# A hybrid decoder block on one core: the first 512 feed-forward features by plain products, earlier loads of f, and two pad tiles that shift operand addresses

## The chip, the core and the metric

The kernel runs on one core of one Trainium2 chip. The metric is the device time of one execution in microseconds (us); lower is better. Times of the kernel before are given as the median of three executions, and one further execution was taken with the hardware profiler. A difference of under about 0.5% of the time cannot be told from no change.

## The reference, cut to what matters

One decoder layer over 512 positions with 2048 features. A state-space mixer and an attention mixer make `y`; the part that the change touches is the channel mixer behind them:

```
x = x + gt1 * (y @ w_out)
h = rmsnorm(x, g_ffn) * (1 + sc2) + sh2
f = (silu(h @ w_gate) * (h @ w_up)) @ w_down      # w_gate, w_up: 2048 x 5632; w_down: 5632 x 2048
x = x + gt2 * f
return rmsnorm(x, g_final)
```

`sh1, sc1, gt1, sh2, sc2, gt2` come from `silu(c) @ w_mod + b_mod`, a matrix of 2048 x 12288 that is read once. Everything is float32. Products are made of two-part operands: each number is written as `hi + lo`, both in the type fp32r, and a product is hi·hi + hi·lo + lo·hi, three matmuls in one PSUM group.

## The kernel before, in words

All activations lie transposed, with 128 features on the partitions and the 512 positions in the row. A **piece** is 128 x 1024 weights: a DMA from the SP queue fetches it (512 KB), ACT writes its `hi` (a cast, 128x1024), DVE writes its `lo` (a subtraction, 128x1024). Five raw buffers (`wraw`) and three pairs of hi/lo buffers (`whl`) go round. TensorE (PE) then does 24 matmuls with a piece of a plain product: 8 tiles of 128 outputs, three matmuls each, with 512 moving columns (lines 190 to 192).

The instructions of each engine are not issued in the order of the text: the framework's scheduler takes, per engine, what is ready, in order of priority, and `high_priority(30)` lifts the splitting of weights. Each engine then runs its list in that fixed order.

**Stage 1, to `run()` at L1119.** w_in (64 pieces), w_glu (8) and w_out (32) are multiplied by `hA`/`hB`, `vv` and `ys`. Beside them DVE does the state-space work, attention, and the product with `w_mod` (L313, one 512 KB DMA `mraw` for each step). `residual` (L1074) adds the w_out product into `x1`, and the 16 tiles of `x1` are stored to DRAM (`x1d`, L1128) to be read back at the end.

**The seam to stage 2.** From the sum of squares, two small PE steps (L361, L379) and a Newton iteration on DVE make the row `r`; ACT copies it to `rbc` (L1214). For each of 16 tiles, DVE (L1225) and ACT (L1226) make the raw `h` in `rawh`. The channel mixer then works on quadrants, 8 tiles by 256 positions: `b11`, `b21`, `b22` are split at once (L1220, L1221), while `t1` to `t4` are sums of quadrants over 128x2048 (L1237 to L1243), split after that.

**Stage 2, gate and up.** 44 blocks (22 groups of 256 features, gate and up) are done by the seven products of a Strassen-Winograd scheme (p1 to p7, in the order p1 p6 p5 p7 p2 p4 p3). A product is 24 matmuls with 256 moving columns (L1273 to L1275), so there are 44 x 7 x 24 = 7392. p1, p2, p3 move `b11`, `b21`, `b22`; p4 to p7 move `t4`, `t1`, `t2`, `t3`. DVE builds the sums of weight quarters (L1188 to L1194) and recombines; `done` (L1279) multiplies silu(gate) by up, splits it in `fo` and stores it to DRAM (`fd`, L1288).

**Stage 3, w_down.** Two passes of 8 output tiles over 44 tiles of f: 88 pieces, 2112 matmuls of 512 columns. Each `f` tile is read back from `fd` by SP (L1336). The last third of the product with w_mod (GT2, 32 steps) runs beside it, one step for each piece, and `x_back` (L1365) reads `x1` again. The last lines scale and store the output.

**Where operands lie.** Pools of `side="right"` are stacked downward from byte 229,344 of each partition, which is 32 modulo 64; the others upward from the left. Pool sizes are multiples of 64 there, so in the program before, `hA`, `hB`, `vv`, `ys`, `b11`, `b21`, `b22` (right) start at 32 modulo 64, and `t1` to `t4`, `f` and all weight tiles `hi`, `lo` (left) at 0 modulo 64.

## Time and profile before

| | us |
|---|---|
| median of 3 executions (lowest, highest) | 2246.65 (2239.68, 2248.37) |
| the profiled execution: its own time | 2242.28 |
| its span, first to last instruction | 2240.2 |
| mean granted TensorE clock | 0.976 |

The profile's page gives busy times, a strip of 40 slices (56 us each) with the busy tenths of each engine and the granted clock, and the costliest groups of instructions. Other views are the windows (busy time, counts and clock between two instants), the timeline (start, duration, instruction, and in brackets the engine's idle time before it with what ended it), and the DMA list. Matmuls are pipelined: a matmul's own duration overlaps the next one's, so the time that one costs is the distance from start to start, or a window divided by its count.

### The profile page before, as it was taken

The numbers are of one execution on the slowest core, as the hardware profiler recorded it, in microseconds if no ns is written. First come the engines' busy times: TensorE is split into PE (matmuls) and PEld (weight loads), VectorE is DVE, ScalarE is ACT, GpSimd is POOL, SyncE is SP. The second block draws the span as 40 slices with busy tenths as digits, with TensorE's granted clock in tenths as the row PEclk, the third lists the DMA queues.
The fourth block names the chain that finished last, engine by engine and source line by source line (L and its number), as shares of the span: only waits on it lengthen the run. The fifth ranks groups of instructions, "written<-read, shape, count | busy, mean of one in ns | idle before, by whom it ended". The sixth has DMA issues, their size and how long they took to land.

```text
span 2240.2 us, 32899 instructions
## 1 busy us (share of the span) xinstructions
PE 2111.2 (94%) x13032; PEld 1879.8 (84%) x13032; DVE 1556.9 (69%) x2275; ACT 864.5 (39%) x1243; POOL 2.0 (0%) x7
## 2 busy tenths in 40 slices
PE   5999999899999929999999999999997999999996
PEld 3878887677777829999999999999997888888885
DVE  7896868967888688788787887878877344232225
ACT  4432443366743254444444444444443121122111
POOL 0000000000000000000000000000000000000000
PEclk9999989999999959999999999999999999999998
DMA  9989786678887404334343343433435988555552
GB/s 358 331 338 178 230 254 196 215 253 277 305 271 266 161 15 131 120 127 141 125 144 121 130 142 123 147 119 130 141 123 196 353 291 303 194 193 191 195 177 75
DMA packets 196561, 435.94 MB, mean 195 GB/s; under 512 B 50036, under 2 KB 70900, under 8 KB 196408
## 3 DMA queue, kind: packets, MB, share of 16 engines
q1 hardware_dynamic: 196168, 433.13, 58.4%
q8 instruction: 102, 1.67, 0.3%
q0 software_dynamic: 240, 0.72, 0.1%
q14 instruction: 51, 0.42, 0.1%
HBM read 380.38 MB, written 53.41 MB: 194 GB/s over the span
## 4 chain that ended last, share of the span: by engine, by line
PE 70%; DVE 10%; DMA 4%; issue 1%; ACT 1%; SPq 0%; DVEq 0%; ACTq 0%
PE g L190 9%; PE g L192 9%; PE g L191 9%; PE y L1273 6%; PE y L1275 6%; PE y L1274 6%; PE z L1273 4%; PE z L1275 4%; PE z L1274 4%; PE x L1275 4%; PE x L1273 4%; PE x L1274 4%; DMA mraw<-in_w_mod 2%; DVE mraw L313 1%; DVE lo L164 1%
## 5 line engine op out<-in xcount | busy, mean ns | idle before, releaser
L164 DVE TENSOR_TENSOR lo<-raw,hi 128x1024 fp32r<-128x1024 f32 x192 | 236.0, 1231 | 348.9 <-ACT hi L160 343.6
L160 ACT CAST hi<-raw 128x1024 fp32r<-128x1024 f32 x192 | 201.7, 1051 | 580.8 <-PE g L191 399.9
L1273 PE MATMUL y<-btt,hi 128*128 128x256 f32 x1056 | 300.0, 284 | 31.9 <-ACT hi L1176 31.5
L1274 PE MATMUL y<-btt,hi 128*128 128x256 f32 x1056 | 299.6, 284 | 0.0
L1275 PE MATMUL y<-btt,lo 128*128 128x256 f32 x1056 | 299.4, 284 | 0.0
L1176 ACT CAST hi<-raw 128x1024 fp32r<-128x1024 f32 x176 | 184.8, 1050 | 285.3 <-PE x L1274 131.7
L190 PE MATMUL g<-f,hi 128*128 128x512 f32 x704 | 275.2, 391 | 12.7 <-DMA f<-fd 12.7
L313 DVE SCALAR_TENSOR_TENSOR mraw<-mraw,cb 128x1024 f32<-128x1024 f32 x192 | 234.1, 1228 | 70.1 <-DMA mraw<-in_w_mod 69.8
L191 PE MATMUL g<-f,hi 128*128 128x512 f32 x704 | 275.0, 391 | 0.0
L192 PE MATMUL g<-f,lo 128*128 128x512 f32 x704 | 274.8, 390 | 0.0
L1177 DVE TENSOR_TENSOR lo<-raw,hi 128x1024 fp32r<-128x1024 f32 x176 | 215.2, 1223 | 80.2 <-ACT hi L1176 80.0
L1273 PEld LDWEIGHTS y<-btt,hi 128*128 128x128 f32 x1056 | 203.0, 192 | 32.5 <-ACT hi L1176 31.8
L1176 ACT CAST hi<-s 128x1024 fp32r<-128x1024 f32 x132 | 138.9, 1053 | 180.9 <-PE y L1274 92.0
L1275 PEld LDWEIGHTS y<-btt,lo 128*128 128x128 f32 x1056 | 203.4, 193 | 0.0
L1274 PEld LDWEIGHTS y<-btt,hi 128*128 128x128 f32 x1056 | 203.4, 193 | 0.0
L1273 PE MATMUL x<-bab,hi 128*128 128x256 f32 x704 | 198.7, 282 | 3.2 <-ACT bab L1220 3.2
L1275 PE MATMUL x<-bab,lo 128*128 128x256 f32 x704 | 199.0, 283 | 0.0
L1274 PE MATMUL x<-bab,hi 128*128 128x256 f32 x704 | 197.6, 281 | 0.9 <-DVE bab L1221 0.9
L1177 DVE TENSOR_TENSOR lo<-s,hi 128x1024 fp32r<-128x1024 f32 x132 | 161.0, 1220 | 12.9 <-ACT hi L1176 12.4
L190 PEld LDWEIGHTS g<-f,hi 128*128 128x128 f32 x704 | 132.8, 189 | 40.7 <-issue 12.9
L192 PEld LDWEIGHTS g<-f,lo 128*128 128x128 f32 x704 | 132.9, 189 | 27.7
L191 PEld LDWEIGHTS g<-f,hi 128*128 128x128 f32 x704 | 132.9, 189 | 27.5
(291 smaller groups left out, 4408.3 us busy)
## 6 DMA issues: line engine op xcount, KB each, us to landing
mraw<-in_w_mod SPq DMA_DIRECT2D x192, 512.0 KB, 6.2
raw<-in_w_gate SPq DMA_DIRECT2D x88, 512.0 KB, 3.4
raw<-in_w_up SPq DMA_DIRECT2D x88, 512.0 KB, 3.9
raw<-in_w_down SPq DMA_DIRECT2D x88, 512.0 KB, 3.8
f<-fd SPq DMA_DIRECT2D x88, 512.0 KB, 3.3
raw<-in_w_in SPq DMA_DIRECT2D x64, 512.0 KB, 5.7
fd<-fo SPq DMA_DIRECT2D x44, 512.0 KB, 4.6
raw<-in_w_out SPq DMA_DIRECT2D x32, 512.0 KB, 5.1
```

The lines of the kernel that those rows point to most:

```text
L160: ACT.copy(hi, p["raw"])
L164: tt(p["hl"][1], p["raw"], p["hl"][0].bitcast(F32), op=ALU.subtract)
L190: PE.matmul(ps, lhs[0], rhs[0], start=first, stop=False)
L191: PE.matmul(ps, lhs[0], rhs[1], start=False, stop=False)
L192: PE.matmul(ps, lhs[1], rhs[0], start=False, stop=last)
L313: stt(raw, raw, 1.0, cb[:, h * (D // 2):(h + 1) * (D // 2)], op0=ALU.mult, op1=ALU.mult, accum_out=macc[:, m, h:h + 1])
L1176: ACT.copy(hi, raw)
L1177: tt(lo, raw, hi.bitcast(F32), op=ALU.subtract)
L1273: PE.matmul(o, hi[:, sl], bh[:, k], start=f, stop=False, skip_group_check=True)
L1274: PE.matmul(o, hi[:, sl], bo[:, k], start=False, stop=False, skip_group_check=True)
L1275: PE.matmul(o, lo[:, sl], bh[:, k], start=False, stop=l, skip_group_check=True)
```

## The change

It has five parts.

1. **Plain products for the first 512 features.** Groups 0 and 1 of gate and up (four of the 44 blocks) leave the Strassen-Winograd list (`NW = 2`). In their place eight PSUM banks collect four tiles of 128 gate features and four of up, over all 16 tiles of h: 16 x 24 = 384 matmuls with 512 moving columns, tile by tile as `h3(k)` makes h. The moving operand is two runs of 256 columns, one from each quadrant, because h is written straight into quadrants `b11`, `b12`, `b21`, `b22`. Each piece comes by four DMAs of 128 KB with rows of 512 bytes.
2. **h and its sums.** `h3` computes from `r` in PSUM (for the first two tiles), writes `hi`, `lo` and, over `x1`, the raw h. `t1`, `t2`, `t4` have tiles of their own; `t3` takes the place of `b12`. The sums and splits stand in the text behind the plain products, but depend on h alone (and `t3` on the plain products of the first eight tiles).
3. **Stores of x1** move into `residual`, four tiles in one DMA.
4. **Stage 3 starts ahead.** Seven loads of f, three pieces of w_down and two of their splits are placed among the last four Strassen products, in the space of `t1` and `t2`. `x_back` moves from entry 4 to entry 35 of the list, behind the GT2 steps.
5. **Addresses.** A tile of 32 bytes (`edge`) at the right end and further ones (`bpad`, `fpad`) shift what is stacked on the right: `hA`, `hB`, `vv`, `ys` come to 0 modulo 64, `f`, now on the right, stays at 0, and all quadrants and `t1` to `t4` are at 32 modulo 64.

The diff, cut to its core:

```diff
+    ctx.enter_context(tc.tile_pool(name="edge", bufs=1, side="right")).tile([P, 8], F32, name="edge")
...
-    mraw = mrx.enter_context(tc.tile_pool(name="mraw", bufs=MR, reuse_waits="tile"))
+    mraw = mrx.enter_context(tc.tile_pool(name="mraw", bufs=MR, side="right", reuse_waits="tile"))
...
             if half:
+                SP.dma_start(x1v[:, fs_[0]:f + 1], x1[0][:, fs_[0]:f + 1])
                 start(sumsq4(ssq, [x1[0][:, f] for f in fs_], cb_ == 0), 1)
...
-    for k in range(KT):
-        SP.dma_start(x1v[:, k], x1[0][:, k])
...
+    def wk_load(k):
...
+        for j, w in enumerate((w_gate, w_up)):
+            for i in range(NW):
+                SP.dma_start(v[:, j, i], w[i, kh, :, :, kk * P:(kk + 1) * P].rearrange("f p c -> p f c"))
...
+    for k in range(4):
+        wk_load(k)
+    r = rsq_psum(ssq, D)
+    wk_prep(0)
+    wk_prep(1)
...
+    open_banks(g=8)
...
+    bb = [bp.tile([P, 2, 2, H, TH], F32R, name=f"b{i}") for i in range(2)]
+    bp.tile([P, 8], F32, name="bpad")
...
+    def h3(k):
...
+        stt(t, x1[0][:, k], gs2[:, k:k + 1], r if k < 2 else rbc, op0=ALU.mult, op1=ALU.mult)
+        hi, lo = [x[:, kh, :, kk] for x in bb]
+        tv = t.rearrange("p (a t) -> p a t", a=2)
+        ACT.activation(hi, tv, AF.Identity, bias=sh)
+        stt(lo, tv, sh, hi.bitcast(F32), op0=ALU.add, op1=ALU.subtract)
+        ACT.activation(x1[0][:, k], t, AF.Identity, bias=sh)
...
-    for i in range(NB):
+    for i in range(NW, NB):
...
+    for k in range(KT):
+        wk_prep(k + 2)
+        if k + 4 < KT:
+            h3(k + 4)
+        if k == KT - 1:
+            prep(0)
...
+        for m in range(8):
+            sl = slice(m * P, (m + 1) * P)
+            mm3(ps[m], (hi[:, sl], lo[:, sl]), (bh, bo), k == 0, k == KT - 1)
+    sg = []
+    for m in range(4):
+        sg.append(st())
+        ACT.activation(sg[m], ps[m], AF.Silu)
+    for m in range(4):
+        tt(sg[m], ps[4 + m], sg[m], op=ALU.mult)
...
+    for m in range(4):
...
+        SP.dma_start(fd[m, :, :S], hi)
+        SP.dma_start(fd[m, :, S:], sg[m])
...
     for n, (bl, p) in enumerate(items):
         prep(n + 2)
+        if n == len(items) - 4:
+
+            t12x.close()
+            ftx.enter_context(tc.tile_pool(name="fpad", bufs=1, side="right")).tile([P, 8], F32, name="fpad")
+            fpool = ftx.enter_context(tc.tile_pool(name="ft", bufs=8, side="right", reuse_waits="tile"))
+            ft.append(fpool)
+            for j in range(7):
+                f_load(j)
+            while at[1] < 3:
+                load_piece(pieces[at[1]])
+                at[1] += 1
+        if n >= len(items) - 2:
+            need(n - len(items) + 2)
...
-    prog.insert(4, x_back)
+    prog.insert(35, x_back)
...
+    g2.append(start(mod_blocks(GT2), 1))
```

## The prediction

> **What bounds the kernel now.** I read the page's strip first.

> ```profile
> span 2240.2 us, 32899 instructions
> ...
> PE   5999999899999929999999999999997999999996
> ...
> PEclk9999989999999959999999999999999999999998
> ```

> PE is busy almost everywhere; the hole in slice 15 (2 tenths, clock at 5) and the notch in slice 31 are the seams into stages 2 and 3. Busy shares say nothing of the distance between matmuls, so I took windows without a hole; count and length give it.

> ```profile
> core 0: us, PE busy (x) PEld busy (x) DVE busy (x) ACT busy (x) POOL busy (x), PEclk, DMA share, GB/s
> 850.00:1700.00 850.00, 849.62 (x7136) 849.33 (x7135) 682.57 (x765) 385.02 (x490) 0.00 (x0) 1.00 0.40 132
> 1750.00:2200.00 450.00, 450.00 (x1987) 372.75 (x1986) 142.76 (x152) 91.60 (x91) 0.00 (x0) 1.00 0.66 227
> 125.00:225.00 100.00, 100.00 (x430) 80.38 (x430) 76.49 (x170) 26.83 (x37) 1.19 (x2) 1.00 0.99 239
> ```

> Stage 2: 850/7136 = 119.1 ns a matmul. Stage 3: 450/1987 = 226.5 ns. Stage 1, same 512 columns, full clock: 100/430 = 232.6 ns. Stages 2 and 3 are PE's alone; stage 1 only in part:

> ```profile
> 350.00:450.00 100.00, 85.54 (x348) 64.89 (x347) 97.89 (x140) 30.55 (x43) 0.00 (x0) 0.98 0.65 214
> ...
> 550.00:700.00 150.00, 144.88 (x741) 117.55 (x741) 126.31 (x290) 82.07 (x162) 0.00 (x0) 1.00 0.84 283
> 700.00:790.00 90.00, 88.66 (x384) 70.74 (x382) 65.55 (x105) 24.20 (x30) 0.00 (x0) 1.00 0.56 190
> ```

> From 350 to 450 DVE is full (97.89 of 100) and PE waits; from 550 to 700 DVE and the DMAs are near their ends (126 of 150, share 0.84); from 700 PE leads again.

> Inside stage 2, the timeline of PE at the starts of three consecutive products:

> ```profile
> 861.75 0.28 PE L1273 MATMUL x<-bab,hi 128*128 128x256 f32 x1
> ...
> 864.58 0.28 PE L1273 MATMUL y<-btt,hi 128*128 128x256 f32 x1
> ...
> 867.46 0.28 PE L1273 MATMUL z<-btt,hi 128*128 128x256 f32 x1
> ```

> 24 matmuls on `bab` (a quadrant, address 32 modulo 64) take 2.83 us, 117.9 ns each; 24 on `btt` (a sum, 0 modulo 64) take 2.88 us, 120.0 ns. Three products of seven of the one kind and four of the other make (3 x 117.9 + 4 x 120.0)/7 = 119.1, the window's number.

> And the seams, again PE's timeline:

> ```profile
> 802.32 0.58 PE L1273 MATMUL x<-bab,hi 128*128 128x256 f32 x1 [3.17 <-ACT bab L1220]
> ...
> 841.87 0.58 PE L1273 MATMUL y<-btt,hi 128*128 128x256 f32 x1 [31.52 <-ACT hi L1176]
> ...
> 1722.42 0.28 PE L1275 MATMUL z<-bab,lo 128*128 128x256 f32 x1
> 1735.44 0.76 PE L190 MATMUL g<-f,hi 128*128 128x512 f32 x1 [12.75 <-DMA f<-fd]
> ...
> 1741.53 0.39 PE L192 MATMUL g<-f,lo 128*128 128x512 f32 x1
> ```

> Stage 2 runs from 802.32 to 1722.54 (last start plus 0.12): 920.2 us for 7392 x 0.1191 = 880.4 us of work; 39.8 us are lost, nearly all behind p1, which is done while p6 waits for `t2`. Then 12.9 us to the first f. The clock of that start, in a window:

> ```profile
> 1735.00:1741.00 6.00, 5.56 (x13) 4.43 (x14) 0.34 (x2) 0.00 (x0) 0.00 (x0) 0.50 1.03 399
> ```

> It is granted 0.50, and the 14 starts from 1735.44 to 1741.53 take 6.1 us instead of 14 x 0.2265 = 3.2: a cold start costs 2.9 us more.

> **The change part by part**, against the profiled execution, 2242.3 us (span 2240.2, 2.1 around it).

> *Stage 1, addresses: -7 us.* The pieces of plain products:

> ```profile
> raw<-in_w_in SPq DMA_DIRECT2D x64, 512.0 KB, 5.7
> ...
> raw<-in_w_out SPq DMA_DIRECT2D x32, 512.0 KB, 5.1
> ...
> raw<-in_w_glu SPq DMA_DIRECT2D x8, 512.0 KB, 5.1
> ```

> (64 + 32 + 8) x 24 = 2496 matmuls, which come from 32 modulo 64, where I read 232.6 ns, to 0, where stage 3 has 226.5: 6.1 ns each, 15.2 us if all were on the path. In the windows 125 to 225 and 700 to 790 they are: about 800 x 6.1 = 4.9 us. Of the other 1,700 (10.4 us) I take a fifth, 2.1, since there a faster PE mostly waits longer for DVE or w_mod. Bounds: 2.5 (half of the sure part) to 15.2. The moves of `mraw` and of the x1 stores I cost at nothing: five raw buffers hold 5 x 24 x 0.2326 = 28 us of PE work, and a store waits for `residual`, eight DVE steps of 512 columns (by the 0.74 us of the L1225 row below, an estimate of 6 us); without that cover each of the four stores would cost these 6 us.

> *Start of stage 2: -1.6 us.* Today's chain behind `r`, on ACT:

> ```profile
> 799.18 0.59 ACT L1214 COPY rbc<-m 128x512 f32<-128x512 f32 x1 [7.32 <-PE m L379]
> 800.59 1.38 ACT L1226 ACTIVATE rawh<-rawh,mod 128x512 f32<-128x512 f32 x2 [0.82 <-DVE rawh L1225]
> 801.88 0.70 ACT L1220 CAST bab<-rawh 128x256 fp32r<-128x256 f32 x2
> ```

> `h3` needs from 799.2 one DVE step (0.74, below) and one ACT step (0.69, half of the x2 row), so PE starts near 800.7, not 802.32.

> *Plain products: +89.3 and a cold start of 2.9.* 384 matmuls of 512 columns. Two runs of 256 at 32 modulo 64 occur nowhere in the trace. Nearest rows: 226.5 and 232.6 ns for 512 in one run, 2 x 120.0 = 240.0 for two matmuls of 256. I take 232.6, the row at the same phase: 89.3 us; bounds 87.0 and 92.2. They run on eight banks without a gap if each tile's inputs come in under 24 x 0.2326 = 5.6 us. What a tile needs, by the groups' means:

> ```profile
> L1177 DVE TENSOR_TENSOR lo<-raw,hi 128x1024 fp32r<-128x1024 f32 x176 | 215.2, 1223 | 80.2 <-ACT hi L1176 80.0
> L1225 DVE SCALAR_TENSOR_TENSOR rawh<-x,gs,rbc 128x512 f32<-128x512 f32 x16 | 11.3, 744 | 2.8 <-ACT rbc L1214 2.8
> L1226 ACT ACTIVATE rawh<-rawh,mod 128x512 f32<-128x512 f32 x16 | 10.9, 717 | 0.8 <-DVE rawh L1225 0.8
> L1176 ACT CAST hi<-raw 128x1024 fp32r<-128x1024 f32 x176 | 184.8, 1050 | 285.3 <-PE x L1274 131.7
> ```

> DVE 1.22 + 2 x 0.74 = 2.7 us, ACT 1.05 + 2 x 0.72 = 2.5 us: half of PE's. Over 90 us DVE has some 46 us left.

> *The sums of h.* They move out of PE's way if the scheduler puts them into that room. Their cost is in DVE's timeline:

> ```profile
> 817.12 2.28 DVE L1237 TENSOR_TENSOR rawh<-rawh 128x2048 f32<-128x2048 f32 x1
> 819.33 1.42 DVE L1221 TENSOR_TENSOR bab<-rawh,bab 128x256 fp32r<-128x256 f32 x4
> ```

> Four sums and four `lo` at 2.28 are 18 us, under the 46. And the second row stands ahead of the first in the text (the loop's last splits), yet runs behind it: the order goes by readiness. So I let p6 find its `t2` ready, and cost the seam behind the plain products at 1.5 us (bounds 0 and 6), for the evacuation of banks and the one weight pair that waits for a buffer. What is late next is that evacuation: four silu, four multiplications, four splits, in the cover of p1 and p6.

> *Stage 2 itself.* 672 Winograd matmuls go (80.0 us); the 6720 left all move operands at 32 modulo 64: 6720 x 0.1179 = 792.3 us. The end comes to 800.7 + 2.9 + 89.3 + 1.5 + 792.3 = 1686.7 against 1722.5: **-35.8 us**. The address term in it is 6720 x 0.0012 = 8.1 us. At 117.9 DVE is still at some 81% (682.57 of 850), so PE stays the bound.

> *Stage 3: -15.3 us.* 12.9 + 2.9 = 15.8 us are lost now; SP's timeline shows why:

> ```profile
> 1725.65 0.33 SPq L1288 DMA_DIRECT2D fd<-fo  x1
> 1726.02 1.57 SPq L304 DMA_DIRECT2D mraw<-in_w_mod  x2
> 1727.69 5.59 SPq L1336 DMA_DIRECT2D f<-fd  x5
> ```

> The f loads stand behind the last store, which waits for DVE. In the change they stand ahead of the last two stores, wait only for p5 and p6 of the last block, and have four products (11.3 us) to land; the tiles asked for are old ones. Behind the waiting loads on SP stand the last weights' loads, all issued by then, and two stores whose f is read 42 pieces later. I leave 0.5 us. The GT2 loads start later but keep one step per piece, and `x_back` has seven pieces, 38 us, before its first use; stage 3 and the tail keep their length.

> **Sum:** 2242.3 - 7 - 35.8 - 15.3 = 2184.2. The median before is 4.4 above the profiled execution, so I predict 2184.2 + 4.4 = 2188.6, say **2188**, against 2246.65.

> [...] The rows differ between the two addresses within one stage and at one clock, so I go by the rows.

> **The rivals.**

> *The shift does nothing.* The two rates might come from something else that differs between the operands: stage 1 has more DVE work beside it, and the `t` tiles lie on the other side. Against: in stage 2 the two kinds alternate every 3 us under the same load, and in stage 3 the rate is 226.5 under a DMA share of 0.66. [...] Price: 7 + 8.1 us, so 2203.

> *The sums come late.* If the scheduler leaves them in the text's order, behind the silu step that waits for the plain products, the old stall returns at a new place: from 817.12 to 841.87 are 24.75 us, less 2.9 under p1, plus 2.9 for a cold clock, less the 1.5 counted: +23, so 2211. Against it stands the order shown above.

> *Slower: the four loads of a piece run in series.* The new loads are small, with 512-byte rows. If each waited for the one before, a piece would take four landings:

> ```profile
> raw<-in_w_gate SPq DMA_DIRECT2D x88, 512.0 KB, 3.4
> ...
> Pd<-kp SPq DMA_DIRECT2D x16, 256.0 KB, 2.3
> ```

> 4 x 2.3 = 9.2 us against PE's 5.6; with a gap in each tile the clock would stay halved (6.1 us for 14 matmuls, 435 ns, as above), so 24 x 0.435 = 10.4 us a tile and 167 us for the stage instead of 92: +75, so 2263, slower than before. It decides from 5.6 us a piece on. Against: a 512 KB load lands in 3.4 us, and SP issued the five f loads within 5.59 us, the last before the first was used at 1735.44; at that pace, 1.1 us, four issues take 4.5 us of the 5.6.

> **How the numbers follow.** My own forecast 0.68; no effect of addresses 0.13; sums late 0.12; serial loads 0.03; something like no gain in both seams 0.04. My own range: 2174 (all of the 15.2, the seam and the plain products at their low ends) to 2203. To hold 8 in 10 it is stretched over the first two rivals: 2174 to 2211. About 0.5% (11 us) is what a measurement can tell from no change, so faster means under 2235: 0.95. Same 0.02, slower 0.03.

> **What would show it.** Right: PE starts the plain products within 13 us of the last w_out matmul; a window inside them has about 233 ns a matmul; all products of stage 2 have 117.9; no idle over 2 us between plain and p6; less than 1 us ahead of the first f; windows in stage 1 at 226.5. Wrong: an idle of 20 us behind p1, `y` products at 120.0, idle PE within the plain products put down to DMA `raw`, or stage 1 as long as before.

## The result, and the profile after

| | before | changed |
|---|---|---|
| median (lowest, highest), 4 runs each | 2245.57 (2239.68, 2248.37) | 2212.3 (2204.14, 2217.67) |
| ratio with 95% interval | | 0.9852 [0.9813, 0.9891] |
| the profiled execution | 2242.28 | 2217.67 |

Faster, by 33 us where I had forecast 58. 2212 lies just outside the range, whose upper end was 2211. The profiled execution of the changed kernel is the highest of its four, so further below each stage is compared by the mean of three profiles.

The page of the changed kernel, the same lines as before; a slice is 55.4 us:

```profile
span 2215.9 us, 32293 instructions
...
PE   5999999989999989999999999999999999999996
...
PEclk9999989999999989999999999999999999999998
```

The hole in slice 15 has shrunk from 2 tenths to an 8, and the notch in slice 31 is gone: both seams closed. What did not happen as forecast shows only in windows, where length divided by count gives the rate (a window also counts the matmuls that reach into it, up to two):

```profile
core 0: us, PE busy (x) PEld busy (x) DVE busy (x) ACT busy (x) POOL busy (x), PEclk, DMA share, GB/s
125.00:225.00 100.00, 100.00 (x443) 82.84 (x442) 76.63 (x171) 26.50 (x36) 1.19 (x2) 1.00 1.00 241
830.00:890.00 60.00, 60.00 (x259) 48.31 (x258) 40.35 (x31) 24.55 (x25) 0.00 (x0) 1.00 0.33 97
920.00:1670.00 750.00, 749.84 (x6337) 749.68 (x6336) 604.99 (x680) 342.08 (x435) 0.00 (x0) 1.00 0.40 133
1720.00:2170.00 450.00, 450.00 (x1930) 362.57 (x1929) 141.43 (x153) 88.61 (x88) 0.00 (x0) 1.00 0.67 228
40.00:780.00 740.00, 698.99 (x3365) 574.99 (x3364) 587.05 (x1124) 314.62 (x551) 1.76 (x3) 0.96 0.80 252
```

First row, stage 1: 443 where before had 430 in the same window; the operands are faster, as forecast. Second, the plain products: 60/259, 232 ns (233.3 from start to start). Third, stage 2: 750/6337 = 118.35 ns, between the forecast 117.9 and the 119.1 of before. Fourth, stage 3: 450/1930 = 233.2 ns, where before needed 226.5. **f has become slow**, although it stayed at 0 modulo 64. The last row is the whole of stage 1, and its clock, 0.96, is lower than that of the same window before:

```profile
40.00:780.00 740.00, 705.98 (x3413) 569.78 (x3412) 594.64 (x1132) 317.72 (x555) 1.76 (x3) 0.99 0.80 255
```

The seams, in PE's timeline of the changed kernel (start, duration, instruction, in brackets the idle time before it and what ended it):

```profile
805.05 1.84 PE L362 MATMUL m<-kct,ssq 128*128 128x1 f32 x8 [4.55 <-DVE ssq L354]
809.41 2.04 PE L380 MATMUL m<-kct,ri 128*128 128x128 f32 x8 [2.52 <-DVE ri L376]
813.05 0.79 PE L191 MATMUL g<-b,hi 128*128 128x512 f32 x1 [1.59 <-ACT b L1188]
...
904.37 0.40 PE L193 MATMUL g<-b,lo 128*128 128x512 f32 x1
904.60 0.28 PE L1393 MATMUL x<-b,hi 128*128 128x256 f32 x1
...
1700.07 0.28 PE L1395 MATMUL z<-b,lo 128*128 128x256 f32 x1
1700.19 0.40 PE L191 MATMUL g<-f,hi 128*128 128x512 f32 x1
```

From the last plain product to p1 are 0.23 us, an ordinary distance. The first f matmul follows the last Strassen product after 0.12 us at an unbroken pace: no wait of 12.75 us, no cold start. The sums of h that p6 waited for now lie under the plain products, in DVE's timeline:

```profile
836.66 2.29 DVE L1286 TENSOR_TENSOR x<-x 128x2048 f32<-128x2048 f32 x1
...
862.70 2.29 DVE L1284 TENSOR_TENSOR b<-x,b 128x2048 fp32r<-128x2048 f32 x1 [0.58 <-ACT b L1283]
```

The sum at 836.66 runs 68 us ahead of p1's start. And SP's timeline shows the f loads issued 11 us ahead of the last stores:

```profile
1689.02 3.74 SPq L1327 DMA_DIRECT2D f<-fd  x7
...
1700.46 0.33 SPq L1408 DMA_DIRECT2D fd<-fo  x1
...
1703.30 0.33 SPq L1408 DMA_DIRECT2D fd<-fo  x1
```

By stage, from the starts of PE's matmuls in three profiles of each kernel (the one above and two more, below):

| us, means of three profiles | before | changed | difference | forecast |
|---|---|---|---|---|
| to the last matmul of w_out | 792.3 | 792.3 | 0.0 | -7 |
| to the first matmul of stage 2 | 13.2 | 12.9 | | |
| plain products | | 91.8 | | |
| Strassen products, with the stall before | 919.9 | 795.7 | -32.7 for the three | -35.8 |
| gap ahead of the first f | 13.1 | 0.1 | | |
| stage 3 | 481.2 | 492.6 | -1.6 for the two | -15.3 |
| tail | 23.0 | 23.0 | 0 | 0 |

The sum is -34.3 against the forecast -58.1; the missing 23.8 us are 13.7 in stage 3, 7.0 in stage 1 and 3.1 in stage 2.

### The profile page after: what moved, and what is told of

Same layout as the page of the kernel before. It is cut to its first block, busy times and chain, and to the rows that moved or that the text cites. A ratio compares the mean times of both kernels' runs of the same rounds, so it can differ in the third digit from the quotient of the medians.

```text
span 2215.9 us, 32293 instructions
## 1 busy us (share of the span) xinstructions
PE 2125.4 (96%) x12744; PEld 1875.8 (85%) x12744; DVE 1518.3 (69%) x2219; ACT 851.5 (38%) x1213; POOL 2.0 (0%) x7
## 4 chain that ended last, share of the span: by engine, by line
PE 72%; DVE 8%; DMA 4%; issue 1%; ACT 1%; SPq 0%; DVEq 0%; ACTq 0%
PE g L191 11%; PE g L193 11%; PE g L192 11%; PE y L1393 5%; PE y L1394 5%; PE y L1395 5%; PE z L1393 3%; PE x L1394 3%; PE x L1393 3%; PE z L1395 3%; PE z L1394 3%; PE x L1395 3%; DMA mraw<-in_w_mod 3%; DVE mraw L314 1%; DVE lo L165 1%
## 5 line engine op out<-in xcount | busy, mean ns | idle before, releaser
L1136 DVE TENSOR_TENSOR lo<-raw,hi 128x1024 fp32r<-128x1024 f32 x176 | 215.3, 1223 | 94.4 <-ACT hi L1135 94.3
L191 PE MATMUL g<-f,hi 128*128 128x512 f32 x704 | 278.4, 396 | 0.0
L192 PE MATMUL g<-f,hi 128*128 128x512 f32 x704 | 278.4, 396 | 0.0
L1135 ACT CAST hi<-s 128x1024 fp32r<-128x1024 f32 x120 | 126.3, 1053 | 165.6 <-PE y L1394 80.9
L1393 PE MATMUL y<-t,hi 128*128 128x256 f32 x640 | 179.9, 281 | 0.2 <-DVE u L1418 0.2
L1394 PE MATMUL y<-t,hi 128*128 128x256 f32 x640 | 179.8, 281 | 0.0
L1395 PE MATMUL y<-t,lo 128*128 128x256 f32 x640 | 179.8, 281 | 0.0
L1394 PE MATMUL x<-b,hi 128*128 128x256 f32 x640 | 179.8, 281 | 0.0
L1395 PE MATMUL x<-b,lo 128*128 128x256 f32 x640 | 179.8, 281 | 0.0
L1393 PE MATMUL x<-b,hi 128*128 128x256 f32 x640 | 179.8, 281 | 0.0
L192 PEld LDWEIGHTS g<-f,hi 128*128 128x128 f32 x704 | 132.4, 188 | 31.9
L1136 DVE TENSOR_TENSOR lo<-s,hi 128x1024 fp32r<-128x1024 f32 x120 | 146.5, 1221 | 16.8 <-ACT hi L1135 16.2
L191 PE MATMUL g<-hB,hi 128*128 128x512 f32 x288 | 115.7, 404 | 12.2 <-DVE rt L883 12.2
L1393 PEld LDWEIGHTS y<-t,hi 128*128 128x128 f32 x640 | 120.6, 188 | 0.3 <-issue 0.3
L1394 PEld LDWEIGHTS x<-b,hi 128*128 128x128 f32 x640 | 120.6, 188 | 0.0
## 6 DMA issues: line engine op xcount, KB each, us to landing
mraw<-in_w_mod SPq DMA_DIRECT2D x192, 512.0 KB, 6.1
raw<-in_w_down SPq DMA_DIRECT2D x88, 512.0 KB, 4.0
f<-fd SPq DMA_DIRECT2D x88, 512.0 KB, 4.3
raw<-in_w_gate SPq DMA_DIRECT2D x80, 512.0 KB, 3.2
raw<-in_w_up SPq DMA_DIRECT2D x80, 512.0 KB, 3.7
raw<-in_w_in SPq DMA_DIRECT2D x64, 512.0 KB, 5.3
fd<-fo SPq DMA_DIRECT2D x40, 512.0 KB, 4.4
raw<-in_w_out SPq DMA_DIRECT2D x32, 512.0 KB, 5.5
```

The costliest lines, as they stand in the source:

```text
L191: PE.matmul(ps, lhs[0], rhs[0], start=first, stop=False)
L192: PE.matmul(ps, lhs[0], rhs[1], start=False, stop=False)
L1135: ACT.copy(hi, raw)
L1136: tt(lo, raw, hi.bitcast(F32), op=ALU.subtract)
L1393: PE.matmul(o, hi[:, sl], bh[:, k], start=f, stop=False, skip_group_check=True)
L1394: PE.matmul(o, hi[:, sl], bo[:, k], start=False, stop=False, skip_group_check=True)
```

## The experiments

My question was what sets the rate of a matmul, since "modulo 64" cannot: f and the operands of stage 1 are both at 0 modulo 64 in the changed kernel, and go at 233.3 and 226.7 ns from start to start. The expectations carry the theories as they stood before each run.

**Where f lies: e1_repeat, e2_f64, e5_f192.** The first is the changed kernel unaltered; the others move f alone, by a larger `fpad` (the changed kernel has f at 128 modulo 256, e2 at 64, e5 at 192, where it also was before).

```diff
-fpad", bufs=1, side="right")).tile([P, 8]      # changed: 32 bytes
+fpad", bufs=1, side="right")).tile([P, 24]     # e2_f64: 96 bytes
+fpad", bufs=1, side="right")).tile([P, 56]     # e5_f192: 224 bytes
```

> The changed kernel once more, unaltered, for the spread of stage 1. In its first profile stage 1 ended (last w_out matmul) at 800.1 us, 11 us later than before, though its instructions stand in the same order on PE and its matmuls run at 226.7 ns in place of 233; the delay came in steps at waits behind which the clock is at half for one or two spells of 3.4 us. Theory G (the faster PE waits longer and so loses the clock more often): again 795 to 802. Theory R (which waits lose the clock is chance): anywhere from 780 to 802, and the granted clock of the timed runs goes with their time.

> fpad made 96 bytes instead of 32: f comes to 64 modulo 128, where the weight tiles lie, in place of 0 modulo 128. Everything else as in the changed kernel. Theory A (512 moving columns are fast only where moving and stationary operand start at the same place modulo 128 bytes): stage 3 back at 226.7 ns a matmul in place of 233.3, 2112 x 6.6 = 14 us less than the changed kernel in the same call. My prediction's rule (modulo 64) says no change, since both are at 0 modulo 64.

> fpad made 224 bytes: f starts at 192 modulo 256, as the hi/lo weight tiles do. All else as in the changed kernel. Theory A2: stage 3 at 226.7 ns a matmul, 478.6 us long in place of 492.6, and the total 14 us under the changed kernel's 2212, near 2198. Theories B2 (own place; before, f was at 192 modulo 256 as well) agrees here; theory C says no change.

Medians: e1 2211.87, ratio to before 0.9838 [0.9814, 0.9862]; e2 2209.49, 0.9836 [0.9811, 0.9862]; e5 **2193.32, 0.976 [0.9733, 0.9786]**. Stage 3 in a window, e2 first, then e5:

```profile
1720.00:2150.00 430.00, 430.00 (x1852) 348.63 (x1851) 134.84 (x145) 85.46 (x85) 0.00 (x0) 1.00 0.65 229
```

```profile
1720.00:2150.00 430.00, 430.00 (x1899) 356.06 (x1898) 136.63 (x146) 88.09 (x87) 0.00 (x0) 1.00 0.66 229
```

430/1852 = 232.2 and 430/1899 = 226.4 ns, beside the same DMA traffic (229 GB/s). All three places are 0 modulo 64, and only one is fast. From start to start, stage 3 of e5 takes 478.5 us against 492.6: 14.1 us, which is 2112 x 6.67 ns. So it is f's address, not the load on the core, that costs the 14 us.

**Stage 1 and the weights: e3_no_edge, e4_weights_shift.** e3 takes the `edge` tile away and gives `bpad` its 32 bytes, so that only the operands of stage 1 go back to their place of before. e4 leaves these and moves the weights: a pad of 64 bytes on the left puts `hi` and `lo` at 0 modulo 256 instead of 192.

```diff
 # e3_no_edge
-    ctx.enter_context(tc.tile_pool(name="edge", bufs=1, side="right")).tile([P, 8], F32, name="edge")
-    bp.tile([P, 8], F32, name="bpad")
+    bp.tile([P, 16], F32, name="bpad")
 # e4_weights_shift, ahead of the pool whl
+    ctx.enter_context(tc.tile_pool(name="lpad", bufs=1)).tile([P, 16], F32, name="lpad")
```

> The 32-byte tile at the right end is left out and bpad made 64 bytes: hA, hB, vv, ys are at 96 modulo 128 as before the change, every address of stages 2 and 3 is as in the changed kernel. Stage 1's matmuls at 233.3 ns again. Theory G: stage 1 ends near 789 as before, 7 to 11 us earlier than in the changed kernel, so a total 7 to 11 us lower. Theory R: stage 1 ends where e1_repeat's does or up to 10 us later, total 0 to 10 us higher.

> A pad of 64 bytes ahead of the hi/lo weight tiles: weights at 0 modulo 128; hA, hB, vv, ys stay at 64, f at 0. Theory A (the relation of the two operands counts): stage 1 slow, 233.3 ns, stage 3 fast, 226.7 ns. Theory B (the moving operand's own place modulo 128 counts): as in the changed kernel, stage 1 at 226.7, stage 3 at 233.3. The prediction's rule (modulo 64): 226.7 in both.

e3: median 2216.86, 0.9867 [0.984, 0.9893]. Stage 1 went back to the count of before:

```profile
125.00:225.00 100.00, 100.00 (x430) 80.42 (x429) 75.74 (x169) 26.53 (x36) 1.19 (x2) 1.00 0.99 240
```

e4, one execution, 2206.83:

```profile
125.00:225.00 100.00, 100.00 (x433) 81.08 (x432) 79.37 (x173) 26.73 (x37) 1.19 (x2) 1.00 0.97 254
...
920.00:1670.00 750.00, 749.96 (x6392) 749.79 (x6391) 611.56 (x686) 344.19 (x437) 0.00 (x0) 1.00 0.38 134
```

Stage 1 lost (443 matmuls to 433) and stage 2 gained (6337 to 6392), while stage 3 stayed at 233.3 ns. In stage 2 no moving operand has changed its place, so the address of the weights counts as well, and a rule on the place of the moving operand alone is out. (The window of stage 1 mixes two kinds: in 16 of the 64 pieces of w_in the weights are the moving operand and `hA` or `hB` the stationary one. Where `hB` moves, at its old place, the spacing from start to start went from 226.7 to 233.3 ns; where the weights move, to 229.0.) None of the rules that I had put down so far gave all three rates, so I measured them by themselves.

**A map: m1_map.** A kernel that computes nothing of the block: the three matmuls of a product on two weight tiles W and two moving tiles M, 96 matmuls for each pair of start addresses, back to back; 512 columns in one run, 256 columns, and 512 in two runs of 256.

```diff
+    def n512(wo, mo):                            # wo, mo: shift of weights and of moving operand, in elements
+        for r in range(4):
+            bh, bo = [t[:, mo + r * S:mo + (r + 1) * S] for t in M]
+            for m in range(8):
+                hi, lo = [t[:, wo + m * P:wo + (m + 1) * P] for t in W]
+                mm3(ps[m], hi, lo, bh, bo, r == 0, r == 3)
...
+    for wo in (0, 16):
+        for mo in range(0, 128, 8):
+            n512(wo, mo)
+        for mo in range(0, 128, 8):
+            n256(wo, mo)
+        for mo in range(0, 128, 8):
+            two(wo, mo)
```

> The disputed price by itself: nothing of the block is computed, only matmul triples (hi.hi, hi.lo, lo.hi, as in the kernel) in a dense stream, 96 for each case: 512 columns in one run, 256 columns, and 512 as two runs of 256; the moving operand's start steps by 32 bytes through 512, the weights lie at 128 and then at 192 modulo 256. The last runs showed that modulo 128 isn't the rule for 512 columns: f and the weights both at 64 modulo 128 ran at 232.4 ns. Theory A2 (the two starts have to agree modulo 256): 226.7 ns at two of the 16 starts for each place of the weights, and these two move by 64 bytes with the weights; 232 to 234 elsewhere; 256 columns run the other way, 120.0 where the starts agree and 115.8 to 118.4 elsewhere. Theory B2 (the moving operand's own place counts): the fast starts stay where they are when the weights move. Theory C (neither; the tile, its neighbours or the traffic beside it count): no pattern in the start.

When the weights were moved by 64 bytes, the whole pattern moved by 64 bytes with them, and it repeats every 256 bytes. What counts is the **distance**: start of the moving operand less start of the stationary one, modulo 256. Mean ns from start to start at full clock:

| distance, bytes | 0 | 32 | 64 | 96 | 128 | 160 | 192 | 224 |
|---|---|---|---|---|---|---|---|---|
| 512 columns, one run or two | 226.7 | 233.3 | 228.9 | 233.3 | 233.3 | 234.3 | 233.3 | 233.3 |
| 256 columns | 120.0 | 117.8 | 117.8 | 120.0 | 118.7 | 117.4 | 113.3 | 118.3 |

The places follow from the pools: weights lie at 192 modulo 256. Before, `t1` to `t4` and f at 192 (distance 0) and the rest on the right at 224 (32). Changed: stage 1 at 192 (distance 0), the quadrants and sums at 160 (224), f at 128 (192). With that the map gives each rate of each kernel so far to within 1 ns: 120.0 and 117.8 before, 118.3 and 233.3 after; in e2, f at distance 128 (232.4 measured); in e4 stage 1 at distance 192, sums at 160 (117.33 measured, 117.4 in the map). It also gives the two kinds in e4's window of stage 1: `hB` on weights is at distance 192 (233.3 measured and in the map), weights on `hB` at 64 (229.0 measured, 228.9 in the map).

**By the map: e10_no_pads, e6_phases.** e10 leaves all three pads out; everything on the right is then at distance 32. e6 puts f at distance 0 and the sums and quadrants at 192, where the map has its fastest 256 columns.

```diff
 # e10_no_pads: the lines of edge, bpad and fpad are removed
 # e6_phases
-    bp.tile([P, 8], F32, name="bpad")
+    bp.tile([P, 16], F32, name="bpad")
-fpad", bufs=1, side="right")).tile([P, 8]
+fpad", bufs=1, side="right")).tile([P, 48]
```

> All three pad tiles left out of the changed kernel: the rest of the change without its part on addresses. Everything on the right starts at 224 modulo 256, 32 bytes behind the weights. By the map: stage 1 and stage 3 at 233.3 ns, stage 2 at 117.8 in place of 118.3, so 3.6 us less in stage 2, stage 3 unchanged, and stage 1 some 5 us longer: total 2212 to 2216, that is, the part on addresses is worth 0 to 4 us as it was written. The prediction's rule (modulo 64) would make stage 3 the same too but cost 15 us in all.

> The map applied: bpad 64 and fpad 192 bytes, so that all quadrants and t1 to t4 start 192 bytes behind the weights modulo 256 (113.3 ns for 256 columns in the map, against 118.3 at the changed kernel's 224) and f at the weights' own place (226.7). All else as in the changed kernel. If the map holds in the kernel: stage 2 shorter by 6720 x 5.0 = 33.6 us, stage 3 by 14 us, total near 2212 - 47 = 2165. Rival: DVE, 81% busy in stage 2 now, becomes late at 84%, and part of the 33 us stays away (total 2175 to 2190, with idle PE put down to DVE or ACT in stage 2).

e10: median **2204.56**, 0.9821 [0.9799, 0.9843]. Its windows of stage 2 and stage 3:

```profile
920.00:1670.00 750.00, 749.88 (x6380) 749.70 (x6379) 609.87 (x684) 344.12 (x437) 0.00 (x0) 1.00 0.39 134
1720.00:2150.00 430.00, 430.00 (x1844) 345.39 (x1843) 134.10 (x144) 85.13 (x85) 0.00 (x0) 1.00 0.66 229
```

Stage 2 at 750/6380 = 117.6 ns, near the 117.9 that I had forecast for the changed kernel, and stage 3 slow at 233.2. The median lies below the 2212 to 2216 expected. It is 7 us below that of the changed kernel (2212.3, and 2211.87 in e1), and the intervals of the ratios overlap: the pads as written were worth nothing, or less. What they brought to stage 1 they lost in stage 2 (795.7 us against 790.1 here, from start to start), and f is equally slow with and without them.

e6: median **2180.15**, 0.9687 [0.9644, 0.973], the fastest median of all, but with runs from 2163.01 to 2194.53. Its profile fell in the slowest run and shows stage 2 at two rates:

```profile
1000.00:1150.00 150.00, 150.00 (x1276) 150.00 (x1276) 121.21 (x136) 68.37 (x87) 0.00 (x0) 1.00 0.39 134
1195.00:1245.00 50.00, 50.00 (x444) 50.00 (x443) 40.02 (x45) 24.54 (x33) 0.00 (x0) 1.00 0.37 128
```

150/1276 = 117.6 and 50/444 = 112.6 ns (start to start 117.8 and 113.3): the same products, the same addresses, the same clock, and PE full in both, so a late DVE, the rival of the expectation, is not what slows it. The quick stretch begins and ends where PE was held up (starts 0.33 and 0.20 us apart at 1192, 0.64 us apart at 1249.6, in place of 0.12). So the map's entry of 113.3 is one of two rhythms. e10 has two as well: its first nine blocks ran at 116.7 ns from start to start, the others, behind starts 0.40 us apart at 1071, at 117.8; its 117.6 is a mean.

**Two rhythms: m2_modes, e11_kick, e12_three_kicks.** m2 computes nothing of the block either; it repeats each distance behind one matmul of 0, 32 to 512 columns. e11 is e6 with one matmul of 96 columns into an unused bank ahead of every p1, e12 has it in the first three blocks alone.

```diff
 # m2_modes
+    for mo in range(0, 64, 8):
+        for n in (0, 32, 64, 96, 128, 160, 192, 224, 320, 384, 448, 512):
+            if n:
+                PE.matmul(ps[7][:, 0:n], W[0][:, 0:P], M[0][:, mo:mo + n], start=True, stop=True)
+            n256(0, mo)
 # e11_kick, on e6_phases, ahead of the products of an item (e12: "and n < 21")
+        if p == "p1":
+            PE.matmul(gps("m")[:, :96], hi[:, 0:P], bh[:, 0, 0:96], start=True, stop=True)
```

> Again nothing of the block, only streams of matmul triples. In e6_phases the 256-column products started 192 bytes behind the weights, where the map had 113.3 ns; they ran at 117.8 for most of stage 2 and at 113.3 from 1193 to 1249 us, switching at two short waits of PE, and its four runs lie 31 us apart. Here each of the eight distances (0, 32 to 224 bytes) is run 12 times, 96 triples of 256 columns (32 of 512: three disturbances), each time behind one odd matmul of 0, 32, 64 to 512 columns. Theory M (two steady rhythms at one distance, chosen by what stood before): at 192 some cases at 113.3 and some near 117.8, at other distances at most one value. Theory N (the kernel's traffic on the memory slows it, not the rhythm): 113.3 in all 12.

> e6_phases with one odd matmul of 96 columns ahead of each block (40 in all, some 50 to 60 ns each, 2.4 us; nobody reads its result). In the streams, at 192 bytes, an odd matmul of 96 columns took the rhythm from 117.8 to 113.3 ns; whether it leaves 113.3 as it is was not seen. If it does: stage 2 at 113.3 ns almost throughout, total 2165 to 2170, runs close together. If each odd matmul turns the rhythm over: 115.5 on average, 2178 to 2182, close together too. If the waits of the kernel decide more than the odd matmul: the spread of e6_phases, 2163 to 2195.

> In e11_kick the blocks ran at 118.2, 118.2, 113.9 ns in a cycle of three odd matmuls. Here only the first three blocks of stage 2 have one, so the third should enter the quick rhythm. If it lasts: stage 2 near 6720 x 0.1135 = 763 us, total 2160 to 2168. If the kernel's waits end it soon: 785 to 790 us and 2178 to 2190, as e6_phases and e11_kick.

In m2 the rate at distance 192 was 113.3 in 5 of 12 cases and 117.8 in 7; at 64 it was 113.3 once and 117.8 else; at 32 116.7 or 117.8, at 160 117.3 or 118.7, at 128 118.7 or 120.0; at 0, 96 and 224 only one (120.0, 120.0, 118.3). With 512 columns each distance had a single rate but for 128, which had 232.4 in three cases and 233.3 in one (233.3 in m1 and e4, 232.4 in e2). No stream changed its rate within its 96 matmuls. Each case ran once, so m2 by itself doesn't show that the odd matmul chooses the rhythm.

e11, median 2187.33, 0.9734 [0.971, 0.9758]: its blocks run in a cycle of 118.2, 118.2 and 113.9 ns (first start of a block to its last), which none of my three cases had. Two neighbouring blocks:

```profile
1006.20:1025.20 19.00, 19.00 (x169) 19.00 (x169) 16.15 (x19) 8.95 (x13) 0.00 (x0) 1.00 0.48 167
1025.40:1044.40 19.00, 19.00 (x163) 19.00 (x163) 14.68 (x18) 8.44 (x11) 0.00 (x0) 1.00 0.32 111
```

The one odd matmul does move the stream from one rhythm to the other, at two of three blocks, through 39 of the 40. e12 was to leave it in the quick one; median 2188.03, 0.9729 [0.9689, 0.9769], and that failed:

```profile
918.00:936.00 18.00, 18.00 (x161) 18.00 (x160) 14.20 (x17) 8.09 (x11) 0.00 (x0) 1.00 0.34 118
1000.00:1650.00 650.00, 650.00 (x5522) 650.00 (x5521) 528.38 (x593) 296.92 (x376) 0.00 (x0) 1.00 0.39 134
```

The second block was quick (18/161, 112 ns), the third odd matmul threw it out again, and 650/5522 = 117.7 ns held to the end. How to reach and keep the quick rhythm on purpose stays open; neither median is below e6's.

**The loads of f: e8_f_late.** The change has the f loads placed four products ahead of the end. e8 places them behind all products instead, as the kernel before did, and keeps the space (that of `t1` and `t2`).

```diff
-        if n == len(items) - 4:
-            t12x.close()
...
-        if n >= len(items) - 2:
-            need(n - len(items) + 2)
...
+    t12x.close()
+    ftx.enter_context(tc.tile_pool(name="fpad", bufs=1, side="right")).tile([P, 8], F32, name="fpad")
+    fpool = ftx.enter_context(tc.tile_pool(name="ft", bufs=8, side="right", reuse_waits="tile"))
```

> One part undone: f's buffers are opened, and its first loads, those of w_down and their splits made, behind the whole of stage 2 instead of among the last four products. My account of the seam (12.9 us of waiting and 2.9 us of half clock in front of stage 3 went away through this move): the seam opens again to 10 to 14 us idle and the cold start, total 13 to 16 us over the changed kernel, near 2227. Rival: the scheduler, which goes by readiness, pulls the loads ahead anyway; then within 3 us of it.

Median 2213.9, 0.986 [0.9839, 0.9881]: no loss that can be told. SP's timeline, then PE's:

```profile
1683.33 0.33 SPq L1327 DMA_DIRECT2D f<-fd  x1
...
1685.93 0.42 SPq L1327 DMA_DIRECT2D f<-fd  x1
...
1699.93 0.33 SPq L1395 DMA_DIRECT2D fd<-fo  x1
1700.31 2.41 SPq L1327 DMA_DIRECT2D f<-fd  x3
```

```profile
1706.18 0.47 PE L191 MATMUL g<-f,hi 128*128 128x512 f32 x1 [0.31 <-DMA f<-fd]
```

Loads that stand behind the stores in the text are still issued ahead of them: the scheduler goes by readiness. All that is left of the place in the text is 0.31 us of waiting. Before, f lay where `t3`, `t4` and the stores' own `fo` had been, which come free last. So that these loads stand earlier in the text is worth nothing that the runs can tell. The space that f takes, which p5 and p6 leave free, is then what most likely opens the seam; that is argued and not shown, since no run puts f back into the old space alone.

**Stage 1's length: e9_before_again, e13_after_third, e14_before_third.** Unaltered kernels, for how far the length of stage 1 goes up and down by itself.

> The kernel before, unaltered, for a second profile of its stage 1. Its first profile had only 20.5 us of half clock in stage 1, the profiles of the changed kernel and its variants 34 to 61 us, whether stage 1's matmuls ran at 233.3 or at 227. Theory R (chance): this one lies among the others, 30 to 55 us, and stage 1 ends at 792 to 798. Theory G (the change brings the half clock): 20 us again and 789.

> The changed kernel a third time, for stage 1. Theory R: half clock in stage 1 between 30 and 61 us, its end between 786 and 801 us, later with more half clock.

> The kernel before a third time, for stage 1. Theory R: half clock between 20 and 60 us; its end, at equal half clock, 5 to 8 us later than the changed kernel's. Theory G: 20 to 34 us again, under all profiles of the changed kernel.

| profile | its time | last w_out matmul | time at half clock until there |
|---|---|---|---|
| before | 2242.28 | 789.1 | 20.5 |
| e9_before_again | 2245.99 | 794.1 | 34.1 |
| e14_before_third | 2245.49 | 793.6 | 37.5 |
| e3_no_edge (stage 1 as before) | 2212.78 | 795.2 | 47.8 |
| changed | 2217.67 | 800.1 | 61.4 |
| e1_repeat | 2206.22 | 788.0 | 41.0 |
| e13_after_third | 2206.77 | 788.9 | 44.4 |

One kernel's stage 1 thus varies by 12 us between executions, most of it by spells of half clock, which come in multiples of 3.4 us (from 3.4 to 20.5). Where one arises is seen at a wait of PE. In the changed kernel's first profile:

```profile
229.25 1.77 PE L191 MATMUL g<-hi,hB 128*128 128x512 f32 x4 [1.91 <-ACT hi L161]
```

and the windows ahead of and behind it:

```profile
226.20:229.60 3.40, 1.49 (x8) 0.91 (x7) 3.08 (x3) 1.29 (x3) 0.00 (x0) 1.00 0.75 223
229.60:236.40 6.80, 6.18 (x15) 4.40 (x14) 6.37 (x9) 2.91 (x5) 0.00 (x0) 0.50 1.05 368
```

1.49 us of work in a stretch of 3.4, then 6.8 us at a clock of 0.50. The same place before:

```profile
228.42 0.50 PE L191 MATMUL g<-lo,hB 128*128 128x512 f32 x1 [1.01 <-DVE lo L164]
```

A wait of 1.01 us, no half clock, and the changed kernel was 4.5 us further behind from here on. The fifteen profiles of the kernels show what half clock goes with: all spells of one profile start on a fixed grid of 3.41 us, nearly all behind a grid stretch in which PE was little busy. Up to 800 us, 132 stretches at full clock had PE busy for less than half; half clock followed 111 of them, and 4 of the 3007 busier ones. So a wait may cost nothing (the 1.01 us before), or 3.4 us and more at half clock (the 1.91 us had 6.8 behind it), by how it falls on the grid.

Over all nine profiles with fast operands in stage 1 it ends at 791.1 on the mean (783.8 to 800.1) with 45.5 us at half clock; over six with slow ones, at 793.8 (789.1 to 796.0) with 36.4. The faster rate thus is there in every run, but gave only 2.6 us of the 15.2 on the mean of the profiles. At equal half clock it gave more: at 34.1, 37.5, 41.0 and 47.8 us of it, where there are profiles of both kinds, stage 1 with fast operands ended 6.2, 10.2, 8.0 and 2.6 us earlier. A straight line through all fifteen, my estimate from these figures, has the end 0.41 us later for each us at half clock and 6.4 us earlier with fast operands (standard error 1.4). Totals agree: e3 differs from the changed kernel in stage 1 alone, and its four runs (mean 2217.3) are 6.0 us above the eight of changed and e1 (mean 2211.2), though the intervals of the ratios overlap. Theory G of the expectations, by which the faster PE makes stage 1 longer, is out: e1 and e13 ended at 788.0 and 788.9, and e3 was not faster. Whether a faster PE itself brings on more half clock, because it empties its work sooner and waits longer, or the six and the nine merely fell so, the runs don't settle: the spells of the two groups overlap (20 to 48 us, 34 to 61), and the two repeats of before came out nearer to the changed kernel (34.1 and 37.5) than its first profile.

## Why the prediction was right and wrong

**Right: the seams.** Both closed by the mechanism given. The sums ran within DVE's room under the plain products, and the rival "the sums come late" is refuted by the sum at 836.66. PE's idle behind the plain products and ahead of f is nil where I had left 1.5 and 0.5 us. The loads of a piece did not go in series: PE has no wait inside the plain products. (That with a wait in each tile the clock would have stayed halved was my estimate. The nearest case in a trace is p1 before: three waits of 0.18 to 0.34 us between its matmuls, and a clock of 0.50 in the window from 802 to 818.) These took 91.8 us where I had summed 92.2 (89.3 and 2.9 of cold start); the rate of two runs of 256 columns at this place, 233.3, was the row I had taken, 232.6. That was in part luck: their distance is 224, not the 32 of that row, and the map happens to have 233.3 at both.

**Wrong, 13.7 us: "stage 3 and the tail keep their length".** This step rested on f staying "at 0 modulo 64", and I costed it at nothing. f moved from distance 0 to distance 192 from the weights, and its 2112 matmuls went from 226.67 to 233.33 ns: 14.1 us, given back all through stage 3. e5, which differs in f's place alone, takes them back, and its median of 2193 lies in the range that I had given my own forecast (2174 to 2203). Against these, gap and cold start brought 15.7 us (13.0 of gap and 481.2 - 478.5 of stage 3) for the 15.3 forecast, which leaves the 13.7.

The failure behind it: in the trace before, every operand at 0 modulo 64 was also at 192 modulo 256, and every one at 32 also at 224. Two places of eight are seen, and I read a rule out of them that the eight don't follow. A third distance, 224, stood unread in the window from 125 to 225: the matmuls in which the weights move, like the one at 228.42 above, have their moving operand at 0 modulo 64 and took 233.3 ns all the same, which no rule on the place of the moving operand gives. The 192 to which f came was nowhere in the trace. My first rival doubted the shift as a cause, and put this doubt as "does nothing"; what it should have priced is that the shift does something else, with f at 2112 x 6.1 = 13 us by the rows I had quoted.

**Wrong, 3.1 us: stage 2 at 117.9.** All 6720 do run at one rate, as forecast, but at 118.33: the sums and quadrants are at distance 224, not 32. 6720 x 0.43 ns = 2.9 us. e10, with everything at distance 32, has 117.6 (116.7, then 117.8).

**Missing, 7 us: stage 1.** The rate moved as forecast, 233.3 to 226.7, and so did the counts in the window from 125 to 225. In the mean of three profiles nothing of it reached the end of the stage. At equal half clock some 6 us did, by the line through the fifteen profiles and by the totals of e3, near the 7 assumed. What the sum put at nothing is half clock behind waits: the three profiles of the changed kernel had 48.9 us of it on the mean, those of before 30.7, and at 0.41 us for each us this estimate takes back 7.5 us. Whether the change brought it on stays open.

**The start of stage 2, -1.6:** behind `r` exactly that (1.59 us of waiting where 3.17 were), but 1.3 us came back one step earlier, at the sum of squares: 4.55 us of waiting where the timeline before has

```profile
792.74 1.84 PE L361 MATMUL m<-kct,ssq 128*128 128x1 f32 x8 [3.21 <-DVE ssq L353]
```

That the stores of x1, now issued from `residual`, are the cause was not tried.

A slip in the sum: the low end of my own range, 2174, should be 2177 by the terms named for it (8.2, 1.5 and 2.3 us off 2188.6).

## What to carry to other kernels

A rate that differs between operands in a trace holds for the places that the trace shows, not for the rule that one reads into them: before moving a buffer, list the start of every operand that moves with it, against that of its partner, and price the ones that land on a place not yet seen. One window in each stage, length by count, shows such a loss, where busy shares (PE was full in stage 3 of both kernels, at 226.5 and 233.2 ns a matmul) say nothing. And the place of a load in the text may matter little, as in e8 (0.31 us of waiting, no loss that can be told): what stood before in its buffer's space is to be looked at first.
